# Three mean squares moved from VectorE to ScalarE, four warm-up products fewer, and residual halves emitted apart, in a two-layer decoder trunk

## The chip, the cores and the metric

The kernel runs on one core of one Trainium2 chip. Its time is the device time of one launch in microseconds (us). A run of the kernel before takes 897.09 us (median of 3 runs, 896.99 to 897.2). Engines are called PE (TensorE), DVE (VectorE), ACT (ScalarE), POOL (GpSimd) and SP (SyncE, which only issues transfers here).

## What is computed

Two layers over 512 tokens of 1024 features. Layer 0 projects the normalized input to two head groups (differential attention and a chunked mLSTM), gates them and projects back; layer 1 is a gated MLP with a 128x128 mixing matrix per channel group. Every layer has one norm ahead of its mixer and one behind it:

```python
def rmsnorm(x, g):
    xf = x.astype(jnp.float32)
    y = xf * lax.rsqrt(jnp.mean(xf * xf, axis=-1, keepdims=True) + EPS)
    return (y * g.astype(jnp.float32)).astype(x.dtype)
...
    h = x
    for l in range(DEPTH):
        pre_g, post_g, params = layers[l]
        hn = rmsnorm(h, pre_g)
        if l % 2 == 0:
            y = even_mixer(hn, l, *params)
        else:
            y = odd_mixer(hn, *params)
        h = h + rmsnorm(y, post_g)
    return h
```

The change touches layer 0's post-norm, layer 1's pre-norm and layer 1's post-norm.

## The kernel before

The 512 tokens are four tiles of 128 (called tokens 0 to 3 here). Every float32 operand of a large product is split into a high part (`wh`, `hT`, cast on ACT) and a low remainder (`wl`, `lT`, subtracted on DVE or POOL), and each product is made of three: high by high, high by low, low by high. The 18 units of layer 0 (`project`, lines 275 and around) walk eight or sixteen blocks of a weight, four tokens each; layer 1 is eight groups (`Group.run`, line 1091) of 512x512 blocks, each made by a Strassen-like scheme of seven phases (P1, P6, P2, P7, Q5, Q4, Q3; group 0 in another order), whose blocks are summed (`U`, L1019), cast (`whg..`, L1032) and subtracted (`wlg..`, L1036).

The order of instructions on each engine is the order in which the program emits them. A counter `clock["t"]` goes up by one with each block of products (`tick`), and `later(dt, fn)` has `fn` emitted `dt` ticks on, so what stands behind what on an engine is set by these numbers. Engines take their queues strictly in order.

**The start.** The first token's input comes in two halves. `warm_up(n)` (L145) puts n products of zeros on PE: four, then two products that spread the pre-norm's gain over the partitions (`gb0`, L151), then five more. Behind them stand the transposes of token 0's first half (`xnT`, L318), which need `xn_a` from DVE (L359); then come the copies `hT` (ACT, L321) and `lT` (DVE, L322), the first real products (`pj`, L275), and the squares of token 1 (ACT, L326).

**A norm's factor.** `sumsq` (L326) squares on ACT and sums into a column. Then DVE makes mean + EPS (one tensor_scalar: L1240 in `f1`, L95 in `rstd_of`, L1492 in `norm`), POOL raises it to the power -1/2 (L1241, L96, L1494), and DVE uses the factor: `residual` adds layer 0's output to `h1` (L1246), `next_norm` squares `h1` and scales it (`xn_b`, L1224), and PE transposes that (`xnT`, L1156).

**The layer boundary.** Layer 0's last unit ends token by token (`f1`); `residual`, `next_norm` and `blocks_of` of each token follow by ticks, among the casts and subtractions for group 0's first blocks (`whg0P`, `wlg0P`), `A11s`, `A12s` and `S3s` (splits of the transposed tokens, L1165 on ACT, L1166 on DVE). POOL also issues the transfers that add one weight block to another (L1012).

**The end.** In the last group's Q4 and Q3 `value` squares a 128x512 bank on ACT and multiplies it by the gain on DVE (L1479); `finish_token` then emits `norm` (L1492, L1494) and `store`: two residual halves on DVE (L1499), each followed by its transfer to `out` (L1501, SP's queue but for the very last half, which goes by ACT's). Q4 finishes tokens 2 and 3, Q3 tokens 0 and 1.

Of the kernel before, what the change touches and what calls it, by code (L numbers as in the profile page):

```python
# [10 lines left out]
F32 = _my.dt.float32  # L11
F32R = _my.dt.float32r
BF16 = _my.dt.bfloat16
AF = _my.ActivationFunctionType
ALU = _my.AluOpType
AX = _my.AxisListType

P = 128
T = 512
NT = T // P  # L20
D = 1024
ND = D // P
EPS = 1e-6
# [33 lines left out]
def hybrid_kernel(tc, x, pre_g0, w_in0, b_ig, b_fg, conv_w, conv_b, lq1, lk1, lq2, lk2,  # L57
                  da_g, ml_g, w_out0, post_g0, pre_g1, w_in1, sg_g, w_sp, b_sp, w_out1,
                  post_g1, out):
    nc = tc.nc  # L60
    x = x[0]
    out = out[0]
# [3 lines left out]
    with ExitStack() as ctx:  # L66
        big = ctx.enter_context(tc.tile_pool(name="big", bufs=1))
        wk = ctx.enter_context(tc.tile_pool(name="wk", bufs=1))
# [9 lines left out]
        def st(n, name):  # L78
            return wk.tile([P, n], F32, name=name, tag=f"st{n}", bufs=6)
# [9 lines left out]
        nc.vector.memset(ones, 1.0)  # L89
        mhalf = wk.tile([P, 8], F32, name="mhalf")  # L90
        nc.vector.memset(mhalf, -0.5)

        def rstd_of(dst, ssum, n, k):

            nc.vector.tensor_scalar(dst, ssum, 1.0 / n, EPS, ALU.mult, ALU.add)  # L95
            nc.gpsimd.tensor_tensor(dst, dst, mhalf[:, :k], ALU.pow)  # L96
# [46 lines left out]
        def warm_up(n):  # L143
            for _ in range(n):
                nc.tensor.matmul(wps, lhsT=warm[:, :P], rhs=warm, start=True, stop=True)  # L145
# [4 lines left out]
        for hf in range(2):  # L150
            nc.tensor.matmul(gb0[hf], lhsT=ones[0:1, :], rhs=grow0[:, hf * 512:(hf + 1) * 512],  # L151
                             start=True, stop=True)
        warm_up(5)
        cols = wk.tile([P, C_N], F32, name="cols")
        dag = wk.tile([P, 1], F32, name="dag")

# [80 lines left out]
        def later(dt, fn, soft=False):  # L237

            clock["due"].append((clock["t"] + dt, fn, soft))
# [84 lines left out]
        def sumsq(dst, src, n=512):  # L324
            junk = wk.tile([P, 1024], BF16, name="junk", tag="junk", bufs=1)
            nc.scalar.activation(junk[:, :n], src, AF.Square, accum_out=dst)  # L326
# [25 lines left out]
        def stats0(i):  # L352
            return rstd0(i, squares0(i))
# [31 lines left out]
        rs = [stats0(0)]  # L385
# [556 lines left out]
        def h1(i, hf):  # L942
            return h1t[i // 2][:, 2 * (i % 2) + hf, :]
# [21 lines left out]
        sp = wk.tile([P, 4, 2], F32, name="sp0")  # L965
# [143 lines left out]
        def new_su(g):  # L1109
            return [wk.tile([P, 2, 512], F32, name=f"{n}{g}", tag="raw", bufs=3)  # L1110
                    for n in ("s1_", "u2_", "u3_")]
# [59 lines left out]
        def blocks_of(i, xn):  # L1171
# [35 lines left out]
            for n, f in enumerate((f0, f1, f2, f3)):  # L1207
                later(R3[i] + 2 * n, f)
# [5 lines left out]
        def next_norm(i):  # L1214
            ss = st(1, f"ts_{i}")
            both = h1t[i // 2][:, 2 * (i % 2):2 * (i % 2) + 2, :]
            sumsq(ss, both.rearrange("p h d -> p (h d)"), 1024)
            rs = st(1, f"rs{i}_b")
            rstd_of(rs, ss, D, 1)

            def f():
                xn = wk.tile([P, 2, 512], F32, name=f"xn{i}_b", tag="mt", bufs=2)
                for hf in range(2):
                    nc.vector.scalar_tensor_tensor(xn[:, hf, :], h1(i, hf), rs, gs[:, 2 + hf, :],  # L1224
                                                   ALU.mult, ALU.mult)
                nc.scalar.dma_start(h1d[i * P:(i + 1) * P, :].rearrange("p (h d) -> p h d", h=2), both)
                blocks_of(i, xn)
            later(R2[i], f)
# [6 lines left out]
        def f1(i, o):  # L1235
            if 0 < i < 3:
                groups[0].sum2(i - 1)
            sumsq(sp[:, i, 1:2], o)
            rs = st(1, f"pr0{i}")
            nc.vector.tensor_scalar(rs, sp[:, i, 1:2], 1.0 / D, sp[:, i, 0:1], ALU.mult, ALU.add)  # L1240
            nc.gpsimd.tensor_tensor(rs, rs, mhalf[:, :1], ALU.pow)  # L1241
            nc.vector.tensor_tensor(y1[:, i, :], o, gb[:, 512:1024], ALU.mult)

            def residual():
                for hf, src in ((0, y0), (1, y1)):
                    nc.vector.scalar_tensor_tensor(h1(i, hf), src[:, i, :], rs, h1(i, hf),  # L1246
                                                   ALU.mult, ALU.add)
                later(RS, lambda: next_norm(i))
            later(1 if i == 3 else 2, residual)
# [11 lines left out]
        ah, al = lambda k: yh[k // 4][:, k % 4, :], lambda k: yl[k // 4][:, k % 4, :]  # L1261
        project("nat", ah, al, f0)
        project("nat", ah, al, f1, tail=TAIL[0], at_tile=first_loads)


# [155 lines left out]
        def minus(d, a, b):  # L1421

            nc.vector.scalar_tensor_tensor(d, a, -1.0, b, ALU.mult, ALU.subtract)

        def ca_of(c, q):
            t, n = {"C11": ("ca", 0), "C22": ("ca", 2), "C21": ("cb", 0), "C12": ("cb", 2)}[c]
            if t not in part:
                part[t] = slot({"ca": "H1", "cb": "M0"}[t], t)
            return part[t][:, n + q, :]
# [24 lines left out]
        h1n = {}  # L1454

        def load_back(t):
            h1n[t] = slot(("W1", "Q8")[t], f"h1n{t}")
            for q in range(2):
                r0 = (2 * t + q) * P
                nc.sync.dma_start(h1n[t][:, 2 * q:2 * q + 2, :],  # L1460
                                  h1d[r0:r0 + P, :].rearrange("p (h d) -> p h d", h=2))

        def chunk1():
            g = 7
            s1, u2, u3 = new_su(g)
            sq = wk.tile([P, 4, 2], F32, name="sp1")

            parts = {}

            def value(c, q, y, to, eng, sign=1.0):  # L1470

                t, n = BLK[c]
                i = 2 * t + q
                sumsq(sq[:, i, n:n + 1], y)
                gain = gb1[:, n * 512:(n + 1) * 512]
                if eng is nc.gpsimd:
                    eng.tensor_tensor(to, y, gain, ALU.mult)
                else:
                    eng.scalar_tensor_tensor(to, y, sign, gain, ALU.mult, ALU.mult)  # L1479
                parts[i, n] = to  # L1480

            def first_half(i, n):

                s_ = sq[:, i, n:n + 1]
                nc.vector.tensor_scalar(s_, s_, 1.0 / D, EPS, ALU.mult, ALU.add)

            def finish_token(i, n, dt):

                rs = st(1, f"pr1{i}")

                def norm():
                    nc.vector.tensor_scalar(rs, sq[:, i, n:n + 1], 1.0 / D, sq[:, i, 1 - n:2 - n],  # L1492
                                            ALU.mult, ALU.add)
                    nc.gpsimd.tensor_tensor(rs, rs, mhalf[:, :1], ALU.pow)  # L1494

                def store():
                    for hf in (1 - n, n):
                        h = h1n[i // 2][:, 2 * (i % 2) + hf, :]
                        nc.vector.scalar_tensor_tensor(h, parts[i, hf], rs, h, ALU.mult, ALU.add)  # L1499

                        (nc.scalar if i == 1 and hf == 1 else nc.sync).dma_start(  # L1501
                            out[i * P:(i + 1) * P, hf * 512:hf * 512 + 512], h)
                later(dt, norm)
                later(2 * dt, store)

            def hook(ph, q, o):
                tt = nc.vector.tensor_tensor
                u2q, u3q = u2[:, q, :], u3[:, q, :]
                if ph == "P1":
                    nc.scalar.copy(s1[:, q, :], o)  # L1510
                elif ph == "P6":
                    tt(o, s1[:, q, :], o, ALU.subtract)
                    tt(u2q, o, ca_of("C12", q), ALU.subtract)
                elif ph == "P2":
                    y = ca_of("C11", q)
                    tt(y, y, o, ALU.add)
                    later(2, lambda: value("C11", q, y, y, nc.gpsimd))
                    later(6, lambda: first_half(q, 0))
                elif ph == "P7":
                    tt(u3q, o, ca_of("C22", q), ALU.subtract)  # L1520
                    tt(o, o, ca_of("C21", q), ALU.add)
                elif ph == "Q5":
                    minus(u3q, o, u3q)
                    tt(o, o, u2q, ALU.add)
                    later(2, lambda: value("C22", q, u3q, u3q, nc.gpsimd))
                    later(6, lambda: first_half(2 + q, 1))
                elif ph == "Q4":
                    value("C21", q, o, ca_of("C21", q), nc.vector)
                    finish_token(2 + q, 0, 2)
                else:  # L1530
                    value("C12", q, o, u2q, nc.vector, -1.0)
                    finish_token(q, 1, 1)
            later(26, lambda: load_back(1))
            later(30, lambda: load_back(0))
            groups[g].run("nat", both(g), hook)

        chunk0()
# [37 lines left out]
```

## Time and profile before

| | |
|---|---|
| median of 3 runs | 897.09 us |
| the profiled execution's own time | 896.77 us |
| its span, first to last instruction | 895.0 us |
| PE busy | 876.2 us (98%) |
| DVE, ACT, POOL busy | 583.3, 486.6, 195.2 us |
| mean granted TensorE clock | 0.995 of full |

The page divides the span into busy time by engine; where PE is busy nearly throughout, time is won only where PE waits, where its clock is low, and ahead of its first and behind its last product. These places are read from the timeline, which gives each instruction's start, its length and, in brackets, how long its engine was idle before it and what released it. PEld is PE's weight load; SPq and ACTq are transfer issues.

### The profile page before, as it was taken

The page shows a single profiled execution, that of the slowest core. Times are in us where ns is not written, and L with a number is a line of the kernel's source. Part 1 is how long each engine was busy: PE and PEld are TensorE (multiplying, and loading weights), DVE is VectorE, ACT ScalarE, POOL GpSimd, SP SyncE. Part 2 cuts the span into 40 slices and gives each one's busy share as a digit, 9 for nine tenths or more (in the row PEclk, how much of TensorE's full clock was granted, in tenths as well). Part 3 has the DMA queues.
Part 4 walks back from the last instruction along what each step waited for, and adds up shares of the span by engine and source line. Part 5 has one row for each costly group of instructions (what it writes and reads, how often), then busy time and mean ns, then how long its engine had stood idle before and what let it go on. Part 6 is the DMA issues. An engine that isn't in the chain of part 4 may idle for free. (4 is left out here: it accounts for less than half of the span.)

```text
span 895.0 us, 12655 instructions
## 1 busy us (share of the span) xinstructions
PE 876.2 (98%) x4740; PEld 743.6 (83%) x4740; DVE 583.3 (65%) x1034; ACT 486.6 (54%) x926; POOL 195.2 (22%) x269
## 2 busy tenths in 40 slices
PE   8999999999999999999999998899999999999996
PEld 5778888887888888887888887778899999998884
DVE  4467745647765576575543228985767676899975
ACT  5424433434666556756543226686756565768642
POOL 3210012431344714544230012011201010101112
PEclk9999999999999999999999999999999999999998
DMA  8223321221222312222236094569776757577952
GB/s 265 73 76 128 98 77 48 71 95 49 72 74 87 97 55 88 71 72 71 93 130 224 1 282 113 125 182 252 192 209 127 227 104 235 107 223 165 257 120 94
DMA packets 57397, 114.80 MB, mean 128 GB/s; under 512 B 4652, under 2 KB 4727, under 8 KB 57208
## 3 DMA queue, kind: packets, MB, share of 16 engines
q1 hardware_dynamic: 42966, 81.73, 27.5%
q0 software_dynamic: 13648, 29.89, 17.2%
q10 hardware_dynamic: 722, 2.36, 0.7%
q8 instruction: 37, 0.61, 0.3%
q14 instruction: 24, 0.20, 0.1%
HBM read 109.78 MB, written 4.20 MB: 127 GB/s over the span
## 5 line engine op out<-in xcount | busy, mean ns | idle before, releaser
L227 DVE TENSOR_TENSOR wl<-raw,wh 128x512 fp32r<-128x512 f32 x126 | 89.7, 730 | 105.7 <-ACT wh L225 105.4
L275 PE MATMUL pj<-wh,hT 128*128 128x512 f32 x320 | 129.0, 403 | 2.0 <-ACT mz L898 1.3
L275 PE MATMUL pj<-wh,lT 128*128 128x512 f32 x320 | 126.3, 395 | 0.0
L275 PE MATMUL pj<-wl,hT 128*128 128x512 f32 x320 | 125.8, 393 | 0.0
L225 ACT CAST wh<-raw 128x512 fp32r<-128x512 f32 x159 | 93.1, 614 | 39.2 <-DMA raw<-in_l_w_out_dram 19.1
L275 PE MATMUL pj<-hT,wh 128*128 128x512 f32 x192 | 77.8, 405 | 0.2 <-ACT mo L881 0.2
L275 PE MATMUL pj<-lT,wh 128*128 128x512 f32 x192 | 75.8, 395 | 0.0
L275 PE MATMUL pj<-hT,wl 128*128 128x512 f32 x192 | 75.8, 395 | 0.0
L275 PEld LDWEIGHTS pj<-wh,lT 128*128 128x128 f32 x320 | 60.5, 189 | 14.3 <-DVE lT L322 0.6
L275 PEld LDWEIGHTS pj<-wh,hT 128*128 128x128 f32 x320 | 60.6, 189 | 14.2 <-ACT mz L898 1.7
L227 POOL TENSOR_TENSOR wl<-raw,wh 128x512 fp32r<-128x512 f32 x34 | 45.5, 1339 | 118.3 <-ACT wh L225 115.7
L275 PEld LDWEIGHTS pj<-wl,hT 128*128 128x128 f32 x320 | 60.5, 189 | 11.2
L1012 POOL DMA_DIRECT2D B<-in_l_w_in_dram x12 | 15.5, 1290 | 203.7 <-DMA B<-in_l_w_in_dram 47.9
L752 ACT ACTIVATE p<-sc,nm 128x512 f32<-128x512 f32 (+3 forms) x64 | 33.8, 528 | 47.3 <-DVE nm L751 45.8
L275 PE MATMUL pj<-wh,yh 128*128 128x512 f32 x128 | 51.2, 400 | 0.0
L275 PE MATMUL pj<-wh,yl 128*128 128x512 f32 x128 | 50.5, 395 | 0.0
L275 PE MATMUL pj<-wl,yh 128*128 128x512 f32 x128 | 50.3, 393 | 0.0
L275 PEld LDWEIGHTS pj<-hT,wl 128*128 128x128 f32 x192 | 36.0, 188 | 8.8
L275 PEld LDWEIGHTS pj<-hT,wh 128*128 128x128 f32 x192 | 36.0, 188 | 8.8 <-ACT mo L881 0.6
L275 PEld LDWEIGHTS pj<-lT,wh 128*128 128x128 f32 x192 | 36.1, 188 | 7.8
L751 DVE TENSOR_REDUCE nm<-sc 128x1 f32<-128x512 f32 (+3 forms) x64 | 31.5, 492 | 2.2
L275 PEld LDWEIGHTS pj<-wh,yl 128*128 128x128 f32 x128 | 24.0, 188 | 5.4
(634 smaller groups left out, 2251.1 us busy)
## 6 DMA issues: line engine op xcount, KB each, us to landing
raw<-in_l_w_in_dram SPq DMA_DIRECT2D x64, 512.0 KB, 3.6
B<-in_l_w_in_dram SPq DMA_DIRECT2D x24, 1024.0 KB, 6.6
B<-in_l_w_in_dram POOLq DMA_DIRECT2D x12, 1024.0 KB, 8.7
raw<-in_l_w_out_dram SPq DMA_DIRECT2D x16, 512.0 KB, 4.3
B<-in_l_w_out_dram SPq DMA_DIRECT2D x8, 1024.0 KB, 9.6
U<-in_l_w_in_dram POOLq DMA_DIRECT2D x5, 1024.0 KB, 8.9
B<-in_l_w_out_dram POOLq DMA_DIRECT2D x4, 1024.0 KB, 10.0
U<-in_l_w_out_dram POOLq DMA_DIRECT2D x2, 1024.0 KB, 10.2
```

Source lines behind the costliest of these rows:

```text
L225: nc.scalar.copy(wh, raw[:, n % 2, :])
L227: eng.tensor_tensor(wl, raw[:, n % 2, :], wh, ALU.subtract)
L275: nc.tensor.matmul(self.outs[i], lhsT=a, rhs=b, start=(n == 0 and m == 0), stop=(n == len(self.ks) - 1 and m == ms[-1]))
L751: nc.vector.reduce_max(nmx[:, c:c + 1], s[:, :nk], axis=AX.X, negate=True)
L752: nc.scalar.activation(pr[:, c, :nk], s[:, :nk], AF.Exp, bias=nmx[:, c:c + 1], accum_out=sm[:, c:c + 1])
L1012: nc.gpsimd.dma_start(self.X[dst], self.block(nm), accum_op=ALU.add)
```

## The change

Three things are changed. First, mean + EPS of layer 0's post-norm, of layer 1's pre-norm and of layer 1's post-norm is made by an activation on ACT (Identity with scale 1/D and the EPS column or the other half's term as bias), right behind the squares there, in place of a tensor_scalar on DVE: twelve instructions, four each. For the pre-norm a column `epsc` is set once. Second, `warm_up(5)` becomes `warm_up(1)`. Third, `finish_token` takes three numbers of ticks, for the norm and for each residual half, and for the very last token the norm is emitted between the squares and the product by the gain.

```diff
+        epsc = wk.tile([P, 1], F32, name="epsc")
+        nc.vector.memset(epsc, EPS)
...
-        warm_up(5)
+        warm_up(1)
...
             rs = st(1, f"rs{i}_b")
-            rstd_of(rs, ss, D, 1)
+            nc.scalar.activation(rs, ss, AF.Identity, bias=epsc, scale=1.0 / D)
+            nc.gpsimd.tensor_tensor(rs, rs, mhalf[:, :1], ALU.pow)
...
             rs = st(1, f"pr0{i}")
-            nc.vector.tensor_scalar(rs, sp[:, i, 1:2], 1.0 / D, sp[:, i, 0:1], ALU.mult, ALU.add)
+            nc.scalar.activation(rs, sp[:, i, 1:2], AF.Identity, bias=sp[:, i, 0:1], scale=1.0 / D)
             nc.gpsimd.tensor_tensor(rs, rs, mhalf[:, :1], ALU.pow)
...
-            def value(c, q, y, to, eng, sign=1.0):
+            def value(c, q, y, to, eng, sign=1.0, between=lambda: None):
...
                 sumsq(sq[:, i, n:n + 1], y)
+                between()
...
-            def finish_token(i, n, dt):
+            def finish_token(i, n, dts):
...
                 def norm():
-                    nc.vector.tensor_scalar(rs, sq[:, i, n:n + 1], 1.0 / D, sq[:, i, 1 - n:2 - n],
-                                            ALU.mult, ALU.add)
+                    nc.scalar.activation(rs, sq[:, i, n:n + 1], AF.Identity,
+                                         bias=sq[:, i, 1 - n:2 - n], scale=1.0 / D)
                     nc.gpsimd.tensor_tensor(rs, rs, mhalf[:, :1], ALU.pow)
 
-                def store():
-                    for hf in (1 - n, n):
-                        h = h1n[i // 2][:, 2 * (i % 2) + hf, :]
-                        nc.vector.scalar_tensor_tensor(h, parts[i, hf], rs, h, ALU.mult, ALU.add)
-
-                        (nc.scalar if i == 1 and hf == 1 else nc.sync).dma_start(
-                            out[i * P:(i + 1) * P, hf * 512:hf * 512 + 512], h)
-                later(dt, norm)
-                later(2 * dt, store)
+                def store(hf):
+                    h = h1n[i // 2][:, 2 * (i % 2) + hf, :]
+                    nc.vector.scalar_tensor_tensor(h, parts[i, hf], rs, h, ALU.mult, ALU.add)
+
+                    (nc.scalar if i == 1 and hf == 1 else nc.sync).dma_start(
+                        out[i * P:(i + 1) * P, hf * 512:hf * 512 + 512], h)
+                for dt, fn in zip(dts, (norm, lambda: store(1 - n), lambda: store(n))):
+                    if dt:
+                        later(dt, fn)
+                    else:
+                        fn()
...
                     value("C21", q, o, ca_of("C21", q), nc.vector)
-                    finish_token(2 + q, 0, 2)
+                    finish_token(2 + q, 0, (1, 3 + q, 4 + 2 * q) if q else (1, 4, 4))
+                elif q == 0:
+                    value("C12", q, o, u2q, nc.vector, -1.0)
+                    finish_token(q, 1, (0, 2, 3))
                 else:
-                    value("C12", q, o, u2q, nc.vector, -1.0)
-                    finish_token(q, 1, 1)
+                    value("C12", q, o, u2q, nc.vector, -1.0,
+                          lambda: finish_token(q, 1, (0, 1, 2)))
```

How this moves instructions is shown at two places. The first is ACT at the layer boundary, tokens 2 and 3 (`ts` are the sums of squares of `h1`, `sp` those of the projection, `pj_3` the bank of token 3). Before:

```order
L1165 CAST A11s<-Af_4233 128x4x128
L326 ACTIVATE junk,ts_4888<-h1b 128x1024
L1180 COPY Af_4234<-xnT_1_4897 128x4x128
L1165 CAST A12s<-Af_4234 128x4x128
L326 ACTIVATE junk,sp_4232<-pj_3_4580 128x512
L1032 CAST whg0P_4935<-B_0_4722 128x1024
L1226 DMA h1d<-h1b 128x1024
L326 ACTIVATE junk,ts_4954<-h1b 128x1024
L1032 CAST whg0P_4963<-B_0_4722 128x1024
```

With the change:

```order
L1167 CAST A11s<-Af_4231 128x4x128
L328 ACTIVATE junk,ts_4886<-h1b 128x1024
L1221 ACTIVATE rs_b<-ts_4886,epsc 128x1
L1182 COPY Af_4232<-xnT_1_4895 128x4x128
L1167 CAST A12s<-Af_4232 128x4x128
L328 ACTIVATE junk,sp_4230<-pj_3_4578 128x512
L1243 ACTIVATE pr_4916<-sp_4230 128x1
L1034 CAST whg0P_4933<-B_0_4720 128x1024
L1229 DMA h1d<-h1b 128x1024
L328 ACTIVATE junk,ts_4952<-h1b 128x1024
L1221 ACTIVATE rs_b<-ts_4952,epsc 128x1
L1034 CAST whg0P_4961<-B_0_4720 128x1024
```

Each sum of squares is now followed by a small activation (L1243 for layer 0's post-norm, L1221 for layer 1's pre-norm), which stands ahead of the copy `Af` and the cast `A12s` of token 2 and ahead of the cast `whg0P` behind token 3's squares. The DVE rows L1240 and L95 are gone, and POOL's queue has the same rows in the same order.

The second place is DVE at the end, from token 3's factor on (`pr` are the factors of tokens 3, 0 and 1 in turn, `bank_4926` and `bank_4927` are the banks of tokens 0 and 1). Before:

```order
L1492 TENSOR_SCALAR pr_8039<-sp_7804 128x1
L1499 SCALAR_TENSOR_TENSOR h1n_7921<-u_7_7803,pr_8039,h1n_7921 128x512
L1499 SCALAR_TENSOR_TENSOR h1n_7921<-cb,pr_8039,h1n_7921 128x512
L1479 SCALAR_TENSOR_TENSOR u_7_7802<-bank_4926,gb_7511 128x512
L1492 TENSOR_SCALAR pr_8065<-sp_7804 128x1
L1499 SCALAR_TENSOR_TENSOR h1n_7944<-ca,pr_8065,h1n_7944 128x512
L1499 SCALAR_TENSOR_TENSOR h1n_7944<-u_7_7802,pr_8065,h1n_7944 128x512
L1479 SCALAR_TENSOR_TENSOR u_7_7802<-bank_4927,gb_7511 128x512
L1492 TENSOR_SCALAR pr_8087<-sp_7804 128x1
L1499 SCALAR_TENSOR_TENSOR h1n_7944<-ca,pr_8087,h1n_7944 128x512
L1499 SCALAR_TENSOR_TENSOR h1n_7944<-u_7_7802,pr_8087,h1n_7944 128x512
```

With the change (token 0's bank is `bank_4924` here, token 1's `bank_4925`):

```order
L1502 SCALAR_TENSOR_TENSOR h1n_7919<-u_7_7801,pr_8037,h1n_7919 128x512
L1483 SCALAR_TENSOR_TENSOR u_7_7800<-bank_4924,gb_7509 128x512
L1502 SCALAR_TENSOR_TENSOR h1n_7919<-cb,pr_8037,h1n_7919 128x512
L1502 SCALAR_TENSOR_TENSOR h1n_7942<-ca,pr_8061,h1n_7942 128x512
L1502 SCALAR_TENSOR_TENSOR h1n_7942<-u_7_7800,pr_8061,h1n_7942 128x512
L1483 SCALAR_TENSOR_TENSOR u_7_7800<-bank_4925,gb_7509 128x512
L1502 SCALAR_TENSOR_TENSOR h1n_7942<-ca,pr_8084,h1n_7942 128x512
L1502 SCALAR_TENSOR_TENSOR h1n_7942<-u_7_7800,pr_8084,h1n_7942 128x512
```

The three rows L1492 are gone from between the products and the residual halves, and token 0's product by the gain (L1483) now stands between the two halves of token 3; on ACT each of the four sums of squares there is followed by its small activation (L1496).

On PE the only difference is that four of the five products of zeros between `gb0` and the first transposes are gone. SP's queue is the same.

## Rows read from the trace of the kernel before

**Rows 1.** The page: PE's busy time, share of the span, instructions.
```profile
PE 876.2 (98%) x4740; PEld 743.6 (83%) x4740; DVE 583.3 (65%) x1034; ACT 486.6 (54%) x926; POOL 195.2 (22%) x269
```

**Rows 2.** Timeline of the start: start us, us, engine, line, operation [idle before <-releaser].
```profile
2.17 0.47 SPq L120 DMA_DIRECT2D x<-in_x_dram  x1
...
6.30 0.75 DVE L359 SCALAR_TENSOR_TENSOR xn_a<-x,rs_a,gb0o 128x512 f32<-128x512 f32 x1 [0.67 <-POOL rs_a L346]
...
6.93 2.31 PE L145 MATMUL wps<-warm 128*128 128x512 bf16 x5
...
9.04 1.06 PE L318 MATMUL xnT<-ident,xn_a 128*128 128x128 f32 x4
...
10.62 1.06 ACT L326 ACTIVATE junk<-x 128x1024 bf16<-128x1024 f32 x1
...
15.33 0.39 PE L275 MATMUL pj<-wh,hT 128*128 128x512 f32 x1
...
15.55 0.39 PE L275 MATMUL pj<-wl,hT 128*128 128x512 f32 x1
...
17.41 0.63 PE L318 MATMUL xnT<-ident,xn_a 128*128 128x128 f32 x4 [0.24 <-DVE xn_a L359]
```

**Rows 3.** DMA issues of 2.1 to 2.6 us: KB each, us to landing.
```profile
x<-in_x_dram SPq DMA_DIRECT2D x1, 512.0 KB, 6.5
```

**Rows 4.** Timeline of DVE around the layer boundary.
```profile
551.66 0.69 DVE L1166 TENSOR_TENSOR A12s<-Af,A12s 128x512 fp32r<-128x512 f32 x1 [0.97 <-ACT A12s L1165]
...
553.41 0.21 DVE L1240 TENSOR_SCALAR pr<-sp 128x1 f32<-128x1 f32 x1
...
556.00 1.42 DVE L1246 SCALAR_TENSOR_TENSOR h1b<-y,pr,h1b 128x512 f32<-128x512 f32 x2 [0.46 <-POOL pr L1241]
...
559.61 1.23 DVE L1036 TENSOR_TENSOR wlg0P<-B,whg0P 128x1024 fp32r<-128x1024 f32 x1 [0.78 <-ACT whg0P L1032]
```

**Rows 5.** Timeline of POOL around the layer boundary.
```profile
554.04 1.31 POOL L1012 DMA_DIRECT2D B<-in_l_w_in_dram  x1 [2.65 <-DVE pr L1240]
554.88 1.08 POOL L1241 TENSOR_TENSOR pr<-pr,mhalf 128x1 f32<-128x1 f32 x1
```

**Rows 6.** Timeline of ACT around the layer boundary.
```profile
558.55 1.03 ACT L1032 CAST whg0P<-B 128x1024 fp32r<-128x1024 f32 x1
```

**Rows 7.** Timeline of PE around the layer boundary: its three waits.
```profile
553.55 0.51 PE L1091 MATMUL bank<-wlg0P,A11s 128*128 128x512 f32 x1 [0.61 <-DVE wlg0P L1036]
...
558.60 0.50 PE L1091 MATMUL bank<-wlg0P,A12s 128*128 128x512 f32 x1 [1.57 <-DVE wlg0P L1036]
...
561.65 1.09 PE L1156 MATMUL xnT<-ident,xn_b 128*128 128x128 f32 x4 [2.32 <-DVE xn_b L1224]
```

**Rows 8.** Windows, 560 to 565 us: busy by engine, granted clock, DMA share, GB/s.
```profile
560.00:565.00 5.00, 3.35 (x13) 2.94 (x14) 4.25 (x7) 2.27 (x5) 0.00 (x0) 0.66 0.82 206
```

**Rows 9.** Waits of PE: waited for, us in total, times, longest us.
```profile
PE bank L1091 <- ACT u L1129: 1.3, 2, 0.9
```

**Rows 10.** Groups of ACT by form: an activation of two columns.
```profile
L514 ACT ACTIVATE ldot<-ldot 128x2 f32<-128x2 f32 x1 | 0.2, 203 | 4.0 <-DVE ldot L513 4.0
```

**Rows 11.** Timeline of the end, all engines.
```profile
884.41 0.19 ACT L326 ACTIVATION_READ_ACCUMULATOR junk<-bank 128x1 f32 x1
...
886.17 0.39 PE L1091 MATMUL bank<-whg7Q,S4s 128*128 128x512 f32 x1
...
887.15 0.19 ACT L326 ACTIVATION_READ_ACCUMULATOR junk<-bank 128x1 f32 x1
...
888.81 0.69 DVE L1479 SCALAR_TENSOR_TENSOR u<-bank,gb 128x512 f32<-128x512 f32 x1
...
889.69 0.54 POOL L1494 TENSOR_TENSOR pr<-pr,mhalf 128x1 f32<-128x1 f32 x1 [2.25 <-DVE pr L1492]
...
890.94 0.74 DVE L1499 SCALAR_TENSOR_TENSOR h1n<-u,pr,h1n 128x512 f32<-128x512 f32 x1
...
891.72 0.35 ACTq L1501 DMA_DIRECT2D out_dram<-h1n  x1
```

## Prediction

> **What bounds the kernel now.** The page comes first: PE is busy 98% of the span [rows 1], so a saving counts only where PE waits, where its clock is low, ahead of its first real product or behind its last. The timeline is then read at the three places that the change touches.
>
> At the start [rows 2] the reader is to see that PE is busy with nothing useful. DVE ends the first half of `xn_a` at 6.30 + 0.75 = 7.05, but the transposes that need it start only at 9.04, because five products of zeros stand in front of them from 6.93 on. They go 0.42 us apart ((9.04 - 6.93) / 5): 512 columns at the lower clock, 1.2 GHz. At 15.33 and 15.55 products go 0.22 apart, at 2.4 GHz. From 17.41 on, where PE waits for DVE once more, it is fed.
>
> At the layer boundary PE waits three times, 0.61, 1.57 and 2.32 us [rows 7], and its granted clock is 0.66 over 560 to 565 [rows 8]: about 3.4 of these 5 us at the lower level, half of full speed. What releases PE there are DVE's subtractions and the scaled token, and these hang on ACT and POOL in turn [rows 4 to 6].
>
> At the end PE issues its last product at 886.17; ACT has the last sum of squares at 887.15 + 0.19 = 887.34; the last residual half ends on DVE at 890.94 + 0.74 = 891.68 and its transfer is issued at 891.72 [rows 11]. These 4.4 us are a chain of small steps on an idle chip.
>
> **Warm-up products.** One product of zeros goes from 6.93 to 7.35, and the transposes follow at once: 9.04 - 7.35 = 1.69 us earlier, 4 x 0.42. Nothing else stops them, since `xn_a` is there at 7.05. Behind them the copies, remainders and token 1's squares move along. The squares start at 10.62 now and would want token 1 at 8.93; its transfer is issued at 2.17 and lands 6.5 us later, at 8.67 [rows 2, 3]. That margin is thin, 0.26 us, but it is there.
>
> What is left of 1.69 us depends on the clock. If it rises at the same moment as now (some 15 us in), 1.69 us more of work runs at the lower level, at 0.22 / 0.42 = 0.52 of the rate, and products alone keep only 1.69 x 0.52 = 0.88. But at 17.41 it was DVE's chain that released PE [rows 2], and that chain moves by the whole 1.69 less the slower transposes of token 1 (a set of four takes 1.06 at the low level, 0.63 at the high one; that set lies mostly ahead of 15 us now already, so about a third of the 0.43 between, 0.15, is lost). I take **-1.5 us**, with 0.88 as the lower end. The upper end: at the boundary the clock was up again after at most 3.4 us of work [rows 7, 8]. Were it so here, work from 7.35 on would bring it up by 10.75; then the transposes take 0.63 and the products ahead of them save some 0.3, so 0.7 more is gained, 2.2 in all.
>
> The Trainium skill bears on this (TensorE: Matmul & The Clock Gate, What's actually happening): the chip samples PE's activity on a beat of its own, which does not begin with the kernel, and the throttled state is the default that activity lifts. By that rule the rise keeps its moment or jumps by a whole beat, but does not slide along with the work; by the row of the boundary it may come earlier. The first gives the 1.5, the second the 2.2; no row here shows the beat, so the nearer case, the start itself, is taken.
>
> **The factors at the layer boundary.** Each small activation on ACT costs about 0.2 us, by the activation of two columns, 0.203 [rows 10]; each tensor_scalar that DVE loses is 0.21 or so [rows 4]. For token 0 the engines are idle and one replaces the other. For tokens 1 and 2 the activation stands ahead of the copy and the cast `A12s`, and DVE waits for exactly that cast (0.97 us of idle ahead of 551.66 [rows 4]): 0.2 us late there, hence `wlg0P` behind it and PE's wait at 553.55. For token 3 the factor itself is made early, yet POOL doesn't use it: in its queue the block addition (L1012, at 554.04) stands ahead of the power, which ends at 554.88 + 1.08 = 555.96 [rows 5], and the residual starts at 556.00 [rows 4]. The addition was released about when L1240 ended; without L1240 it comes at most 0.2 earlier, but behind a `wlg0P` that is 0.2 later. I call that -0.1. Last, token 3's second activation stands ahead of the cast `whg0P` at 558.55 [rows 6], for which DVE idles 0.78 us until 559.61 [rows 4]; L95, which it replaces, lay inside that idle time and was free. So 0.2 more. Sum: 0.2 + 0.2 - 0.1 = **+0.3 us**, a small loss. Upper bound 0.85 (three tokens, each 0.2 and two hops of 0.04 between engines, all on the path); lower bound -0.3 (if the power isn't held up, DVE's 0.46 of idle ahead of 556.00 goes, less 0.2 for `whg0P`). PE's waits for ACT further on, 1.3 us [rows 9], would swallow a PE that is late there, so the clock's dip is costed at nothing; without that cover it is worth up to about as much.
>
> A page speaks against this part. The Trainium skill (ScalarE: Activation LUTs, Rules for kernel authors) wants 0.3 us budgeted for an activation with a pointer as bias, where the row shows 0.2 without one. With 0.3, three places on the path (two here, one at the end) would make the sum 0.3 us smaller.
>
> **The end.** Now from the last sum of squares (887.34) to the power on POOL (889.69) 2.35 us pass: DVE is still at token 0's residuals, then makes token 1's product by the gain (888.81 to 889.50) and only then the mean square [rows 11]. With the change the activation follows the squares on ACT: 0.2 us and a hop between engines (0.03 from 559.58 on ACT to 559.61 on DVE, 0.04 from POOL to DVE at 556.00 [rows 4 to 6]; 0.07 is taken, twice as much), so the power starts at 887.61, **2.08 us** earlier. It ends at 888.15. DVE must then be free: the product by the gain can start with the end of the squares, 887.36 to 888.05, and token 0's residuals are done before: its squares end at 884.60 [rows 11], 0.2 + 0.07 + 0.54 later is 885.4, and behind token 3's second half DVE needs until about 887.3. The last pair of halves takes as long as now (from the power's end, 890.23, to 891.68), to 889.6, and the transfer and the tail are the same. Moving token 3's halves apart costs nothing, since its factor is long ready by then. Bounds 1.9 (0.1 more for the activation and a hop) and 2.2.
>
> **Sum.** -1.5 + 0.3 - 2.1 = -3.3 us on the profiled execution's 896.77, which lies 0.3 below the median of 897.09; against the median that is 893.8. The rest of the kernel is bound by PE and has its loads issued as buffers come free, so it should pass the start's gain on.
>
> **The rivals.**
> (a) *The clock rises earlier.* For it: the boundary's quick rise [rows 7, 8]. Against it: at the start the transposes and products from 9.04 did not bring it up before some 15 us. 0.7 more: 893.1.
> (b) *The start's gain is swallowed*, by token 1's transfer (0.26 us of margin) or the ones behind it, which keep their absolute times while everything else moves up. Then 0.3 - 2.1 = -1.8 remains: 895.3. Against it: only the first microseconds hang on transfers [rows 2].
> (c) *The boundary gains*: POOL's power isn't held up by the block addition, -0.3 in place of +0.3: 893.2. Against it: the queue's order is unchanged.
> (d) *Slower: the clock stays low.* The four products of zeros did keep PE at work; if it is their absence that delays the rise, every us of work at the lower level costs 1 - 0.52 = 0.48. It decides from 3.3 / 0.48 = 7 us on, that is if the rise comes after 22 us in place of 15; at 30 us the price is 7.2 and the time 897.1 - 3.3 + 7.2 = 901.0. Against it: the real products now start earlier and follow each other without a gap, and at the boundary the clock rose with no such help.
> (e) *ACT gains nothing at the end*: were the activation to start only when DVE's product by the gain has ended, 0.7 of the 2.1 would be lost: 894.5. The order shown contradicts it.
>
> **How the numbers follow.** Forecast 0.52, (a) 0.15, (b) 0.13, (c) 0.09, (d) 0.03, (e) 0.08. The likeliest time is 893.8. The range takes in (a) and (c) below and (b) above with the terms' bounds: 892.5 to 895.5. A difference of 0.2%, 1.8 us, is about what a measurement of this kernel can tell from none; faster by more than that means under 895.3. That holds for all but (d) and a good half of (b) and the bad ends of the terms together: faster 0.86, the same 0.11, slower 0.03.
>
> **What would show it.** Transposes of token 0 at about 7.4, the DVE wait at 17.41 moved to about 15.9. At the boundary PE's three waits about as long as now, POOL's power for token 3 still behind the block addition. At the end the power starting some 0.3 us behind the last squares, and from the last product's issue to the span's end some 6.7 us in place of 8.8 (895.0 less 886.17). It is wrong if products are still 0.42 apart beyond 16 us, if the boundary moves by over 1 us, or if DVE is late for the last factor.

## The result, and the profile after

The change takes 902.01 us (median of 5, 901.2 to 902.18) against 897.09 for the kernel before (896.89 to 897.68): a ratio of 1.0051, interval 1.0039 to 1.0063. It is slower by some 4.9 us, where 893.8 was forecast and 895.5 was the upper end of the range. The profiled execution took 901.32 us, 4.55 more than that of before.

The start went as forecast. Timeline of the start of the change (start us, us, engine, line, operation), which answers to [rows 2]:

```profile
6.93 0.61 PE L147 MATMUL wps<-warm 128*128 128x512 bf16 x1
7.34 1.06 PE L320 MATMUL xnT<-ident,xn_a 128*128 128x128 f32 x4
...
14.79 0.63 PE L277 MATMUL pj<-wh,lT 128*128 128x512 f32 x1
...
15.21 0.43 PE L277 MATMUL pj<-wh,hT 128*128 128x512 f32 x1
...
15.48 0.39 PE L277 MATMUL pj<-wl,hT 128*128 128x512 f32 x1
...
15.95 0.49 PE L320 MATMUL xnT<-ident,xn_a 128*128 128x128 f32 x3
```

Transposes start at 7.34 in place of 9.04, and those that stood at 17.41 stand at 15.95: 1.46 us gained. Products go 0.42 apart up to 15.21, then 0.27, so in these two executions the rise from 1.2 to 2.4 GHz came at about the same moment (0.22 apart from 15.33 [rows 2]) and did not slide along with the work. That it was the same moment is luck. The run e2 below starts like the kernel before, with five products of zeros, and in its profiled execution products have the length that belongs to 2.4 GHz, 0.40, from 11.10 on, where the kernel before has 0.63. Timelines of PE, before first, then e2:

```profile
11.36 0.63 PE L275 MATMUL pj<-wl,hT 128*128 128x512 f32 x1
```
```profile
11.10 0.40 PE L277 MATMUL pj<-wl,hT 128*128 128x512 f32 x1
...
16.89 0.63 PE L320 MATMUL xnT<-ident,xn_a 128*128 128x128 f32 x4 [0.25 <-DVE xn_a L361]
```

So did the end. Timeline of the end of the change, which answers to [rows 11]:

```profile
892.76 0.39 PE L1093 MATMUL bank<-whg7Q,S4s 128*128 128x512 f32 x1
...
893.68 0.20 ACT L328 ACTIVATION_READ_ACCUMULATOR junk<-bank 128x1 f32 x1
...
893.90 0.29 ACT L1496 ACTIVATE pr<-sp 128x1 f32<-128x1 f32 x1
894.27 0.54 POOL L1498 TENSOR_TENSOR pr<-pr,mhalf 128x1 f32<-128x1 f32 x1 [2.26 <-ACT pr L1496]
...
896.30 0.34 ACTq L1504 DMA_DIRECT2D out_dram<-h1n  x1
```

The power starts 0.39 us behind the last squares (893.88 to 894.27), in place of 2.35. From the last product to the span's end 899.6 - 892.76 = 6.84 us pass, in place of 895.0 - 886.17 = 8.83 [rows 11]: 1.99 gained. But that last product is issued 6.59 us later than before, and the start was 1.46 ahead: 8.05 us were lost in between.

At the boundary (waits of PE, 545 to 580 us; timelines of ACT and PE there), which answers to [rows 6, 7]:

```profile
PE xnT L1158 <- DVE xn_b L1227: 2.7, 1, 2.7
PE bank L1093 <- DVE wlg0P L1038: 2.2, 2, 1.4
```
```profile
560.72 0.29 ACT L1221 ACTIVATE rs_b<-ts,epsc 128x1 f32<-128x1 f32 x1
560.92 1.03 ACT L1034 CAST whg0P<-B 128x1024 fp32r<-128x1024 f32 x1
```
```profile
564.02 0.63 PE L1158 MATMUL xnT<-ident,xn_b 128*128 128x128 f32 x4 [2.65 <-DVE xn_b L1227]
```

PE's waits are 2.2 in two and 2.65, against 0.61 + 1.57 and 2.32 [rows 7]: 0.3 more. That is not the loss either. The page shows where it sits: PE's busy time, to set beside [rows 1].

```profile
PE 883.7 (98%) x4736; PEld 746.7 (83%) x4736; DVE 581.9 (65%) x1023; ACT 490.5 (55%) x938; POOL 196.4 (22%) x269
```

Four products fewer, and PE is busy 7.5 us longer. The same stretch of layer 0 in both timelines, the first of 30 products that read wh or wl and load hT or lT as weights, and the instruction behind them; before first, the change second. (In these rows the operand that is read, 128x512, stands first and the one that is loaded, 128*128, second: their order, wh,hT then wl,hT then wh,lT, is that of the pairs in `Unit.mm` with `lhsT`, the loaded operand, from hT or lT.)

```profile
338.68 0.39 PE L275 MATMUL pj<-wh,hT 128*128 128x512 f32 x1
...
345.56 0.61 PE L782 MATMUL ao<-dv,q 128*128 128x128 f32 x4
```
```profile
339.21 0.40 PE L277 MATMUL pj<-wh,hT 128*128 128x512 f32 x1
...
346.22 0.61 PE L784 MATMUL ao<-dv,q 128*128 128x128 f32 x4
```

(345.56 - 338.68) / 30 = 229 ns, (346.22 - 339.21) / 30 = 234 ns. There is no wait in either stretch and no lower clock (0.39 to 0.40 is the length of a product at 2.4 GHz in both): each product costs some ns more, and the loss grows all through the kernel. The change is 1.46 ahead at 16 us, 0.53 behind at 339, 2.37 behind at the transposes of the boundary (561.65 [rows 7], now 564.02), 6.59 behind at the last product.

### The profile page after: what moved, and what is told of

Its sections match the earlier page's. It is cut to its first block, busy times and chain, and to the rows that moved or that the text cites. A ratio compares the mean times of both kernels' runs of the same rounds, so it can differ in the third digit from the quotient of the medians.

```text
span 899.6 us, 12651 instructions
## 1 busy us (share of the span) xinstructions
PE 883.7 (98%) x4736; PEld 746.7 (83%) x4736; DVE 581.9 (65%) x1023; ACT 490.5 (55%) x938; POOL 196.4 (22%) x269
## 4 chain that ended last, share of the span: by engine, by line
PE 91%; DVE 4%; ACT 3%; issue 1%; POOL 0%; DVEq 0%; POOLq 0%; ACTq 0%
PE pj L277 48%; PE bank L1103 18%; PE bank L1093 14%; PE ao L784 2%; PE vs L1336 2%; PE sc L748 1%; PE sc L750 1%; PE at L772 1%; PE yT L855 1%; PE mN L656 1%; PE mN L658 1%; PE mU L662 1%; ACT junk L328 1%; DVE wlg0Q L1038 1%; PE xnT L320 1%
```

## The experiments

What can make every product slower? The diff's first two lines, which the prediction passes over: epsc is a new tile. The pool lays its tiles in the order of creation, one of 4 bytes takes a slot of 32, and all later tiles of that pool move 32 bytes on, wh and wl, the products' operands, among them. Theory: layout. Rivals: ACT's added work slows the products; the missing products of zeros put the stream in another phase.

**The tile taken away, two ways; the tile alone; the warm-up alone.**

```
e1: -epsc = wk.tile([P, 1], ...)   +epsc = mhalf[:, 7:8]
f1: -epsc = wk.tile([P, 1], ...)   +cols = wk.tile([P, C_N + 1], ...); epsc = cols[:, C_N:]
e2 (before): +epsc = wk.tile([P, 1], F32); nc.vector.memset(epsc, EPS)
e4 (before): -warm_up(5)           +warm_up(1)
```

> The change whole, but EPS lies in the unused eighth column of mhalf, so that no tile is added and every tile behind mhalf lies where it lay in the kernel before. Layout theory (the 32 bytes that epsc takes push the products' operands wh and wl to other addresses, and products that read them go some ns further apart): products at the old spacing again, so 902.0 less some 8, about 894, and the three terms of the prediction show in full. ACT theory (the activations moved to ACT, or the order of work that they bring, slow the products): still about 902. Warm-up theory (fewer products of zeros put the whole stream in another phase): still about 902.

> The change whole, with EPS in a 60th column of cols, whose slot has room for it: again no tile more, every tile where it lay in the kernel before, and the whole computation as in the change. Layout theory: 894.0, as with EPS in mhalf. It is the base for the runs that follow.

> The kernel before with nothing changed but the tile epsc and its memset, which nothing reads. Layout theory: about 897.1 + 8 = 905, products at the spacing of the change. ACT theory and warm-up theory: 897.1, since neither ACT's work nor the warm-up is touched.

> The kernel before with four warm-up products fewer and nothing else changed; no address changes. Layout theory and the prediction's term: 897.1 - 1.5 = 895.6. Warm-up theory (the loss of some 8 us comes from here): about 903.6.

Measured: e1 894.0 (ratio 0.9967, 0.9954 to 0.9979; in it the eighth column of mhalf, an exponent in one of layer 0's norms, is EPS in place of -0.5). f1 893.98 (0.9968, 0.9957 to 0.9980). e2 904.42 (1.0082, 1.0068 to 1.0096). e4 895.62 against 897.07 (0.9984, 0.9975 to 0.9993). The layout theory has all four within 0.6 us; both rivals fall. The tile costs 8.0 us in the change and 7.4 alone; the warm-up gains 1.45. f1 is the change without its accident, and the base of what follows. Its 30 products, in its timeline, take (343.99 - 337.11) / 30 = 229 ns again:

```profile
337.11 0.39 PE L277 MATMUL pj<-wh,hT 128*128 128x512 f32 x1
...
343.99 0.61 PE L784 MATMUL ao<-dv,q 128*128 128x128 f32 x4
```

**Which tiles.**

```
f2: -junk = wk.tile([P, 1024], BF16, ...)   +junk = wk.tile([P, 1040], BF16, ...)
f3: -mhalf = wk.tile([P, 8], F32, ...)      +mhalf = wk.tile([P, 16], F32, ...)
    dag = wk.tile([P, 1], ...) moved behind the first raw
g3: between the first wh and the first wl: +gap = wk.tile([P, 1], F32, ...)
```

> The base with junk 32 bytes wider: wh, wl, raw and all that follows lie 32 bytes further on, as in the change, while the tiles ahead of them (warm, rows, the transposes' input, cols) stay. Theory of the products' own operands (wh and wl at 32 bytes off a multiple of 64): 902, the change's time. Theory of the tiles ahead (inputs of small work on other engines): 894.

> The base with mhalf 32 bytes wider and dag laid behind raw: the tiles ahead of wh lie 32 bytes further on, as in the change, while wh, wl and raw stay. Theory of the products' own operands: 894. Theory of the tiles ahead: 902.

> The base with a tile of 32 bytes between wh and wl: wl and raw lie 32 bytes further on, wh stays. If each product's spacing follows from the place of its own operand: products with wl slow down by 3 to 4 ns, those with wh alone stay; wl is in a third of them, so about a third of the 7.4 us, 896.5. If only the wh tiles count (or raw): 894.0, or the full 901.4.

Measured: f2 901.39 (1.0049, 1.0036 to 1.0063), so wh, wl and the tiles behind them carry 7.4 of the 8.0. f3 895.53 (0.9983, 0.9974 to 0.9992): neither 894 nor 902. The spacing of layer 0's products is that of the base; the 1.5 us come behind the boundary. In the profiled executions f3 is 0.4 ahead of the base at 561 us and 0.5 behind at 584 (the granted clock over 550 to 570 us is 0.83 in f3, 0.91 in the base), and it loses 1.4 more from 727 to 796. There the same 48 products of 256 columns go (790.77 - 785.33) / 48 = 113 ns apart in the base and (792.73 - 787.08) / 48 = 118 in f3, though neither of their operands has moved. What slows them is open. So the place of a product's own operands is not all that its spacing hangs on. PE's timelines, base first:

```profile
785.33 0.39 PE L1103 MATMUL bank<-S3s,whg5P 128*128 128x256 f32 x2
...
790.77 0.39 PE L1103 MATMUL bank<-S1s,whg5Q 128*128 128x256 f32 x2
```
```profile
787.08 0.40 PE L1103 MATMUL bank<-S3s,whg5P 128*128 128x256 f32 x2
...
792.73 0.40 PE L1103 MATMUL bank<-S1s,whg5Q 128*128 128x256 f32 x2
```

g3 897.88 (1.0006, 0.9997 to 1.0015): 3.9 more than the base, where a third of 7.4 was expected. Moving wl alone is enough to lose half.

**The other two terms on the base.**

```
g1: finish_token and the two calls for C12 as in the kernel before
g2: -nc.scalar.activation(rs, ss, AF.Identity, bias=epsc, scale=1.0 / D)   +rstd_of(rs, ss, D, 1)
    and the factor pr0 on DVE again
```

> The base (EPS in cols, all tiles in their old places) with the end as in the kernel before: mean squares on DVE, both residual halves together. The prediction's term for the end: 894.0 + 2.1 = 896.1 (896.0 by the 2.0 us that the two traces differ there). If the end's gain were an accident of the layout: 894.0.

> The base with the factors of layer 0's post-norm and layer 1's pre-norm on DVE again, as in the kernel before. The prediction's term (the move to ACT costs 0.3 us there): 893.7. Rival (c), the boundary gains by the move: 894.3. Nothing at all: 894.0.

Measured: g1 896.09 (0.9988, 0.9979 to 0.9997): the end is worth 2.11 us. g2 893.33 (0.9958, 0.9945 to 0.9970): the move to ACT costs 0.65 at the boundary by the medians (the base's six times lie between 893.56 and 895.16); in the profiled executions g2 has its transposes at 560.19 and the base at 560.45, 0.26 later. In the base an activation of 0.29 stands ahead of the cast of whg0P, and DVE waits 1.40 for that cast, 0.78 in g2 (timelines: ACT of the base, DVE of the base, DVE of g2):

```profile
557.16 0.29 ACT L1221 ACTIVATE rs_b<-ts,cols 128x1 f32<-128x1 f32 x1
557.36 1.03 ACT L1034 CAST whg0P<-B 128x1024 fp32r<-128x1024 f32 x1
```
```profile
558.42 1.23 DVE L1038 TENSOR_TENSOR wlg0P<-B,whg0P 128x1024 fp32r<-128x1024 f32 x1 [1.40 <-ACT whg0P L1034]
```
```profile
558.16 1.23 DVE L1038 TENSOR_TENSOR wlg0P<-B,whg0P 128x1024 fp32r<-128x1024 f32 x1 [0.78 <-ACT whg0P L1034]
```

**Place or distance.** In the built kernels wh begins at byte 172480 of each partition before and at 172512 in the change; hT, from another pool, at 65664 in both. The first is a multiple of 64, the second is not: a theory of place. The distance is 417 x 256 + 64 before and 417 x 256 + 96 in the change: a theory of distance. From here on "distance" is the remainder of wh's byte less hT's by 256. Against the base e3 moves wh 64 on, f4 wh 96, g4 hT 64 and wh 128, h1 both 32, h2 hT 64, h3 hT 32.

```
e3 (the change): -epsc = wk.tile([P, 1], ...)   +epsc = wk.tile([P, 16], ...)
f4: -junk = wk.tile([P, 1024], BF16, ...)   +junk = wk.tile([P, 1072], BF16, ...)
g4: ahead of hT: +gap1 = big.tile([P, 16], F32, ...)   behind lT: +gap2 = big.tile([P, 16], F32, ...)
    -nlam = wk.tile([P, 1], ...)   +nlam = cols[:, C_N + 1:C_N + 2]
h1: ahead of all other tiles: +shift = big.tile([P, 1], F32, ...)
h2: -mhalf = wk.tile(...)  -dag = wk.tile(...)   +mhalf = big.tile(...)  +dag = big.tile(...)
h3: -mhalf = wk.tile(...)   +mhalf = big.tile(...)
```

> The change whole, with epsc 64 bytes wide in place of the slot of 32. Layout theory, if what counts is whether the operands begin at a multiple of 64 bytes: about 894, as without the tile; if a multiple of 128 counts too, better than that (wh then begins at a multiple of 128, which it does not in the kernel before). ACT and warm-up theories: about 902.

> The base with junk 96 bytes wider: wh and wl begin 32 bytes behind a multiple of 128, the one of the four places in 128 bytes not tried yet (the kernel before has 64, the change 96, the run with 64 bytes for epsc 0). If only a multiple of 32 against 64 counts: 902, as the change. If the place within 128 bytes counts by itself, anything from 894 to 902.

> The base with the tiles of the slots H0 to H3 (hT and lT, the products' other operands, and what takes their slots later) moved from a multiple of 128 bytes to 64 behind one, where wh and wl lie; all else in its old place within 128 bytes. If the place of the 128 columns that are loaded as weights counts by itself (64 good, 0 bad): products that load hT and lT come down from 233 to some 229.5 ns, those that load wh and wl stay at 229.5, about 892. If the two operands must lie at different places in 128 bytes (as with 64 bytes for epsc, where both lay at 0): products that load wh and wl go up from 229.5 to some 232.5, about 898.

> The base with a tile of 32 bytes ahead of all other tiles: each of them lies 32 bytes further on, so wh and wl stand where the change has them (32 bytes off a multiple of 64), but their distance to hT, lT and the other operands is that of the kernel before. Theory of the place (an operand at 32 bytes off a multiple of 64 is read more slowly): 901.4 or more. Theory of the distance (what counts is how the two operands of a product, or those of neighbouring products, stand to each other): 894.0.

> The base with mhalf and dag laid into the other pool, ahead of hT: hT, lT and the tiles behind them lie 64 bytes further on, wh and wl stay, so both kinds of operand lie at 64 behind a multiple of 128, and at the same place within 256 bytes. Theory of the place: as in the run with hT and lT alone at 64 (898.7), where both kinds also lay at 64. Theory of the distance: another time than that, since there the two kinds lay 128 bytes apart within 256 and here 0; which one is not forecast by it, between 890 and 904.

> The base with mhalf alone laid into the other pool: hT, lT and the tiles behind them lie 32 bytes further on, wh and wl stay, and the distance between the two kinds is 32 bytes in place of 64. Theory of the place, for the tiles of weights alone: products that load wh and wl keep 229.5 ns, those that load hT and lT change. Theory of the distance: both kinds change; time not forecast, between 890 and 904.

Where these expectations tell products that load wh or wl from those that load hT or lT, the two are the wrong way round: it is the products that load hT and lT that go 229 apart in the base, and those that load wh and wl that go 233.

The 30 products again, in the timelines of h1, g4 and h3, one fence each:

```profile
337.20 0.39 PE L279 MATMUL pj<-wh,hT 128*128 128x512 f32 x1
...
344.08 0.61 PE L786 MATMUL ao<-dv,q 128*128 128x128 f32 x4
```
```profile
337.18 0.39 PE L277 MATMUL pj<-wh,hT 128*128 128x512 f32 x1
...
344.17 0.61 PE L788 MATMUL ao<-dv,q 128*128 128x128 f32 x4
```
```profile
337.94 0.39 PE L277 MATMUL pj<-wh,hT 128*128 128x512 f32 x1
...
344.94 0.61 PE L784 MATMUL ao<-dv,q 128*128 128x128 f32 x4
```

All runs, by distance; ns is the mean of these 30, taken in the same way:

| distance | runs | ns | us (median) | ratio, interval |
|---|---|---|---|---|
| 0 | h2 | 228 | 895.03 | 0.9980, 0.9970 to 0.9989 |
| 32 | h3 | 233 | 901.08 | 1.0044, 1.0031 to 1.0057 |
| 64 | f1; h1 | 229; 229 | 893.98; 893.99 | 0.9968; 0.9969, 0.9956 to 0.9981 |
| 96 | the change; f2 | 234; 233 | 902.01; 901.39 | 1.0051; 1.0049 |
| 128 | e3; g4 | 232; 233 | 899.65; 898.73 | 1.0028, 1.0017 to 1.0038; 1.0021, 1.0012 to 1.0030 |
| 160 | f4 | 234 | 903.27 | 1.0073, 1.0061 to 1.0086 |

The ns belong to the distance named; the us hold more than that. In h2 the slots ahead of hT, layer 1's S3s and S4s among them, have moved by 32 only, and its granted clock over 550 to 570 us is 0.83, against 0.91 in the base. Both fit a time 1 us above the base's in spite of closer products in layer 0, but the parts were not measured one by one.

h1 decides: all tiles 32 bytes on, wh where the change has it, and the time is the base's to 0.01 us. Place is out, that of either operand alone: hT begins at the same byte in h1 and h3, wh at the same byte in f1 and h3, and the spacings are 229, 233 and 229 (h1, h3, f1). A multiple of 64 for wh is neither needed (h1) nor enough (e3). The same distance by two ways gives the same spacing to 1 ns (e3 and g4), and h3 loses 7.1 us without moving wh at all.

**Forecasts from the rule.** mv0 is 64 bytes larger than its neighbours, so creating it ahead of hT in place of behind brings the slots of hT and lT, and no other, to distance 0 (in layer 1 these slots hold A11s and A12s, among others). Both versions stand on g2.

```
i1: mv = [new_mv(0)] moved ahead of hT = [...]
i2: ahead of q8 = ...: +mv_0 = slot("W0", "mv0", F32, (P, 4, 2, 258))
    ahead of xp = ...: +dv_0, klb_0 = slot("V0", "dv0"), slot("V1", "klb0", F32R)
```

> The version with the boundary's factors on DVE (893.3), with the tile mv0, 64 bytes larger than its neighbours, created ahead of hT and lT in place of behind them: these four lie 64 bytes further on and so at distance 0 from wh and wl within 256 bytes; nothing else moves. Theory of the distance: layer 0's projections go 228 ns apart, as in the run at distance 0, where that had brought 3.1 us by 380 us of the span; so 890, with what the slots H0 and H1 hold in layer 1 not forecast. Theory of the place (the loaded weights' own): about 898, as with hT and lT at 64 before.

> The same version with mv0 created ahead of all other tiles of its pool, and two more tiles created ahead of xp, the other tile of that larger size: all slots but those of mv0 and xp lie at distance 0 from wh and wl within 256 bytes. Theory of the distance: most of some 4000 products come from a mean of 231 to 228 ns, about 11 us: 882. If distance 0 helps only where hT and lT are read: 890, as the run before. Theory of the place: about 898.

Measured: i1 891.23 (0.9936, 0.9923 to 0.9948), near the 890 expected, far from 898. i2 891.77 (0.9939, 0.9925 to 0.9952), 10 us above what was expected of it. PE's timelines say why: the boundary's transposes and the last product, in g2, i1 and i2, one fence each.

```profile
560.19 0.63 PE L1158 MATMUL xnT<-ident,xn_b 128*128 128x128 f32 x4 [2.31 <-DVE xn_b L1226]
...
884.73 0.39 PE L1093 MATMUL bank<-whg7Q,S4s 128*128 128x512 f32 x1
```
```profile
556.94 0.76 PE L1158 MATMUL xnT<-ident,xn_b 128*128 128x128 f32 x4 [2.31 <-DVE xn_b L1226]
...
882.65 0.39 PE L1093 MATMUL bank<-whg7Q,S4s 128*128 128x512 f32 x1
```
```profile
555.58 1.08 PE L1160 MATMUL xnT<-ident,xn_b 128*128 128x128 f32 x4 [2.31 <-DVE xn_b L1228]
...
883.45 0.39 PE L1095 MATMUL bank<-whg7Q,S4s 128*128 128x512 f32 x1
```

At the boundary i1 is 3.25 us ahead of g2 and i2 4.61; at the last product 2.08 and 1.28. So distance 0 holds for layer 0's other operands too, by less than the 11 us that I had multiplied out, and layer 1 gives 3.3 of it back in i2. Not all of that is spacing: product by product, i2's lead over g2 falls from 4.6 us to 3.7 between 553 and 571 us of g2's span (granted clock over 550 to 570 us: 0.83 in i2, 0.91 in g2), from 4.2 to 0.2 between 639 and 806, and is 1.3 at the end. From 639 to 806 lie the products that load wh or wl and read 256 columns of the other operand. A stretch of these in the timelines of g2 and i2 (a row of x2 and one of x1 alternate):

```profile
700.12 0.40 PE L1103 MATMUL bank<-S3s,whg3P 128*128 128x256 f32 x2
...
705.07 0.40 PE L1103 MATMUL bank<-S3s,whg3P 128*128 128x256 f32 x2
```
```profile
699.86 0.40 PE L1105 MATMUL bank<-S3s,whg3P 128*128 128x256 f32 x2
...
702.74 0.40 PE L1105 MATMUL bank<-S1s,whg3Q 128*128 128x256 f32 x2
```

4.95 us for 42 products is 118 ns, 2.88 for 24 is 120: here distance 0 is the worse one. i1, which leaves most of these alone, is by the medians the fastest version that was run, 5.9 us under the kernel before; i2's five times, 890.88 to 892.1, lie around i1's, 891.13 to 891.44.

## Why the prediction was wrong

Its terms were right, its list of parts was not.

- **Warm-up products, -1.5.** Measured alone -1.45 (e4). The transposes came at 7.34, as forecast. That the clock rose at its old moment was luck in this pair of executions, and the term does not hang on it: in e2 the rise came at least some 4 us earlier, and the transposes of 17.41 stand at 16.89, 0.5 earlier, where rival (a) had 0.7. The Trainium skill's rule weighed there (TensorE: Matmul & The Clock Gate, What's actually happening), that the beat does not begin with the kernel, agrees with this: the same start saw the rise at about 15 us before and by 11.1 in e2.
- **Boundary, +0.3.** +0.65 by medians, +0.26 between two profiles, inside the bounds given. The power for token 3 stayed behind the block addition (556.82 behind 555.98 on POOL). The places were right, `A12s` and the cast of whg0P behind the activations: PE's three waits are 0.89, 1.42 and 2.66 in the base against 0.61, 1.59 and 2.31 in g2, so the first and the third, where the two losses of 0.2 were put, are longer by 0.28 and 0.35, and the second is shorter by 0.17. The activation was mis-sized: 0.29 us, not 0.2. The Trainium skill (ScalarE: Activation LUTs, Rules for kernel authors), which budgets 0.3, agrees.
- **End, -2.08.** -2.11 (g1), 1.99 between the profiles.
- **Sum, -3.3.** The change without the tile's displacement (f1) measures 893.98 against 896.98: -3.0. By the 0.3 per activation of the Trainium skill (ScalarE: Activation LUTs, Rules for kernel authors) the estimate would have been just that.
- **The step that failed** is the sentence "The rest of the kernel is bound by PE and has its loads issued as buffers come free, so it should pass the start's gain on". It takes the products' spacing as given, as does the prediction's first sentence (a saving counts only where PE waits, where its clock is low, or at the two ends): it was PE's busy time itself that moved, from 876.2 to 883.7 us. The tile epsc, which the diff adds in its second line, was costed at nothing without a word: one memset off the path. Its memset is indeed nothing; the 32 bytes that it takes cost 8.0 us (902.01 - 893.98).
- **The rivals.** The slower one, (d), had 0.03, a time near the right one (901.0) and the wrong mechanism: the granted clock is 0.996 on the mean, as before. None of the others covers a product that is slower at full clock without a wait, and neither does the list of what would make the prediction wrong. Products are not 0.42 apart beyond 16 us and DVE is not late for the last factor; the boundary's transposes do come 2.37 us later, but the boundary's own waits grew by 0.3 only, and the rest came from the spacing ahead of it.

Open: why the distance matters. That two reads of one product or of neighbouring ones meet would fit, but no view shows it. A period longer than 256 bytes does not show: at 96, 128 and 160 the products whose operands stand 256, 512 or 768 bytes further apart have the same mean spacing to 0.5 ns. Nor is the distance of a product's own operands everything: f3 moves none of them and has 118 ns where the base has 113.

## What to carry to other kernels

Where PE is busy nearly all the time, a new tile is an edit of every tile created behind it: put a small constant into a spare column of a tile that exists (or create its tile last, which was not tried here), and compare the spacing of a long run of equal products in the two traces before any other explanation. When a small edit changes the time by more than its parts can, move all tiles together and then one pool against the other; and once it is known that distance counts, choose it, as i1 does with one line moved.

## What the runs showed of the hardware that was not expected

- Products of 128 rows by 512 columns at 2.4 GHz are 227 to 234 ns apart with no wait shown, depending on how the bytes of one operand stand to those of the other. Counted as the byte of the operand that is read less that of the one that is loaded, remainder by 256, the means over all such products of layers 0 and 1 (the outer tenths left out) are: 0: 227 to 228 (i2, h2); 32: 233 (h3); 64: 230 (f1); 96: 233 (the change); 128: 232 (e3); 160: 234 (f4); 192: 233 (f1); 224: 233 (h3).
- Counted so, the role of a tile does not matter: products that load hT or lT and those that load wh or wl have the same mean to 0.5 ns at 0 (i2, h2), 128 (e3) and 192 (f1). In f1 products that load hT and read wh stand at 64 and go 229 apart; those that load wh and read lT stand at -64, that is 192, and go 233 apart. In h2 both stand at 0: the first go 228 apart (the table), the second 227. Two rows each, 9 products apart, f1 (2.10 / 9) and then h2 (2.04 / 9):

```profile
299.81 0.39 PE L277 MATMUL pj<-lT,wh 128*128 128x512 f32 x1
...
301.91 0.39 PE L277 MATMUL pj<-lT,wh 128*128 128x512 f32 x1
```
```profile
297.15 0.39 PE L277 MATMUL pj<-lT,wh 128*128 128x512 f32 x1
...
299.19 0.39 PE L277 MATMUL pj<-lT,wh 128*128 128x512 f32 x1
```

- Products that read 256 columns want another distance: 113 or 118 ns at 192 (the base and f3; 118 in the stretch of g2), 120 at 0 (i2).
- The clock's rise at the start has no fixed moment: about 15 us into the span before and in the change, by 11.1 in e2, whose start is that of the kernel before.
